# The end of a two-layer encoder: where the last range's squares are added, and what stands behind the last residual sums

## The chip, the core and the metric

The kernel is one program on one NeuronCore of a Trainium2 chip. The metric is the time of one execution in microseconds on the device. Five engines work side by side, each through its own list of instructions in a fixed order: TensorE (PE, with its weight loads shown apart as PEld), VectorE (DVE), ScalarE (ACT), GpSimd (POOL) and SyncE (SP), whose list here holds only the starts of transfers. An instruction that needs another engine's result waits for a semaphore, and everything behind it on its own engine waits with it. TensorE writes its results into PSUM, a small memory of eight banks here; the rest lies in SBUF.

## The reference

Two inputs, a prompt of 256 tokens and a sample of 512, go through the same two layers of width 1024. Layer 0 mixes with an mLSTM in both directions, layer 1 with sliding-window attention; after each mixer comes a gated feed-forward with a convolution of width 3. What matters for this case is the end: the last feed-forward's residual sum, and then the final norm, which is the output.

```python
def rmsnorm(x, g):
    xf = x.astype(jnp.float32)
    y = xf * lax.rsqrt(jnp.mean(xf * xf, axis=-1, keepdims=True) + EPS)
    return (y * g.astype(jnp.float32)).astype(x.dtype)

def trunk(x, c, ...):
    for l in range(DEPTH):
        ...
        h = rmsnorm(x, norm_g[l, 1]) * (1 + sc2) + sh2
        x = x + g2 * conv_ffn(h, ffn_w_up[l], ffn_conv_w[l], ffn_conv_b[l], ffn_w_down[l])
    return rmsnorm(x, final_g)
```

## The kernel before, in words

All 768 tokens are kept transposed: 128 partitions hold a part of the 1024 features, there are eight such parts ("squares" and "tiles" c = 0 to 7 below), and tokens run along the free axis. The residual stream `xt` is two slabs of four parts each (c 0 to 3 in the first, c 4 to 7 in the second). At the end of the last layer the tokens are treated as three ranges of 256: RANGES[0] and RANGES[1] are the sample's halves, and the last one, RANGES[2], is the prompt. I call them the first range, the other range and the last range.

The last stage of the feed-forward's down product (function `down` in `ffn`, with p = NPART - 1) goes through the three ranges. For each c of a range, `tile` makes six matmuls of 128 x 256 (three for each of two chunks of the inner dimension: weights and activations are each split into a high and a low half) into one PSUM bank, and `resid` (L606, VectorE) multiplies them by the gate and adds them to `xt`. `square` (L111, ScalarE) then squares the new `xt`. After the eighth c the range's norm runs as a generator, `Norm.stages`, that is advanced while the next range's tiles are written, by a clock of estimated microseconds (`tick`).

The norm of a range needs the sum of squares over the eight parts and over 128 partitions. The first two ranges add six of the eight squares on VectorE (L120) into one tile; TensorE then sums the remaining three tiles over the partitions by a matmul whose weights are the squares and whose moving operand is two columns of 1/1024 (`inv`). These are the row sums; L136 and L266 in the rows with `pa<-inv,nt`. For the last range nothing is added before: all eight squares go to TensorE one by one (L136). One square's row sum is two matmuls, one for each 128 tokens, and each of them appears as two records in the trace, so four records for a square.

Then a small chain follows. The mean plus epsilon is copied out of PSUM (L159 on VectorE, L157 on ScalarE for the last range), GpSimd raises it to the power -1/2 (L160), and TensorE spreads the factor of each token over all 128 partitions by a product with the identity (`spread`; rows `pa<-kct,nr`, two matmuls and four records). The last range spreads twice, into two banks, so that ScalarE and VectorE each read their own. ScalarE copies the factor to SBUF (L588). Then each of the eight parts is scaled (function `output`): most by one VectorE instruction (L596), the others by ScalarE with the weight g (L593) and by GpSimd with the factor (L594). Each part is stored to HBM when it is scaled (L598): 24 stores of 128 KB, on SP's queue but for four of the last range's, which ScalarE starts.

The `pa` tiles rotate through four PSUM banks, and the `ps` tiles are four more banks that are used in turn. A tile that finds its bank unread must wait for the reader. The order of each engine's list is not the order in which the code is written: a scheduler with a timeline of its own estimates sets it when the program is built, and can put any instruction ahead of another that it doesn't depend on. `issue_after(x)` tells it to put nothing of a block ahead of instruction x.

## Time and profile before

| | us |
|---|---|
| median of 3 runs | 1822.28 |
| lowest and highest of them | 1821.72, 1824.81 |
| profiled execution | 1823.43 |
| its span, first to last instruction | 1821.6 |
| PE busy in it | 1788.2 (98%) |
| DVE busy | 1387.4 (76%) |
| ACT busy | 890.9 (49%) |
| POOL busy | 475.2 (26%) |

The span is 1.83 us shorter than the profiled execution's own time, which also holds what lies ahead of the first and behind the last instruction. TensorE is busy almost throughout, and the change touches only what happens after about 1801 us. So the page's sums say little about it, and the views that follow are those of the last 25 us: the chain of work that ended last, the rows of each engine in order of time, and the busy times by stretch with the clock that TensorE was granted. A row of an engine's timeline has the start in us from the span's start, the time from the first start to the last end, the engine, the line, the operation, what it writes and reads, the shape, and the count; in brackets how long the engine stood idle before it, and what ended that.

### The profile page before, as it was taken

What the parts mean: (1) busy time and instruction counts of PE and PEld (TensorE: products, weight loads), DVE (VectorE), ACT (ScalarE), POOL (GpSimd) and SP (SyncE); (2) the same over time, 40 slices, a digit from 0 to 9 for tenths busy, and PEclk for the clock granted to TensorE, in tenths of its full rate; (3) what the DMA queues carried; (4) which work ended last, traced back from release to release, by engine and by line L of the source; (5) the groups of instructions that cost most, each with busy time, mean ns of one, the idle gap of its engine ahead of it and who ended that gap; (6) DMA issues with size and microseconds to landing.
All of it is one profiled execution on the core that took longest, in us unless ns stands there. A gap on an engine that the chain in (4) does not pass through costs nothing.

```text
span 1821.6 us, 28983 instructions
## 1 busy us (share of the span) xinstructions
PE 1788.2 (98%) x11290; PEld 1653.4 (91%) x11290; DVE 1387.4 (76%) x2148; ACT 890.9 (49%) x1798; POOL 475.2 (26%) x386
## 2 busy tenths in 40 slices
PE   7999999999999999999999999999999999999998
PEld 4988888889998999999999999989989999999997
DVE  4876676786799777787877867767998777777776
ACT  4553343444465444444444657665564444444443
POOL 2100000031024333333331313320244333333321
PEclk9999999999999999999999999999999999999998
DMA  9334565547212122222123321133122222222212
GB/s 339 122 120 147 175 225 172 193 163 228 79 56 81 59 70 70 70 68 66 65 70 95 106 92 42 62 98 128 47 81 70 70 70 70 70 71 70 70 36 70
DMA packets 64245, 184.48 MB, mean 101 GB/s; under 512 B 6167, under 2 KB 23831, under 8 KB 64108
## 3 DMA queue, kind: packets, MB, share of 16 engines
q1 hardware_dynamic: 63532, 182.11, 30.6%
q8 instruction: 89, 1.46, 0.3%
q10 hardware_dynamic: 576, 0.52, 0.1%
q14 instruction: 48, 0.39, 0.1%
HBM read 176.17 MB, written 6.43 MB: 100 GB/s over the span
## 4 chain that ended last, share of the span: by engine, by line
PE 86%; DVE 5%; ACT 4%; DMA 2%; issue 1%; POOL 1%; SPq 0%; POOLq 0%; DVEq 0%; ACTq 0%
PE ps L266 27%; PE pa L266 24%; PE ps L1353 10%; PE ps L1356 10%; PE ps L1354 10%; PE pa L1192 1%; DMA raw<-in_w_dram 1%; ACT whi L272 1%; DVE wlo L273 1%; PE ps L432 1%; DVE ada L528 0%; DMA raw<-in_adaln_w_dram 0%; PE pa L1353 0%; PE pa L1354 0%; DVE wlo L1478 0%
## 5 line engine op out<-in xcount | busy, mean ns | idle before, releaser
L272 ACT CAST whi<-raw 128x1024 fp32r<-128x1024 f32 x231 | 241.8, 1049 | 342.2 <-PE pa L266 143.3
L273 DVE TENSOR_TENSOR wlo<-raw,whi 128x1024 fp32r<-128x1024 f32 x231 | 315.5, 1367 | 114.6 <-ACT whi L272 112.3
L266 PE MATMUL pa<-slab,whi 128*128 128x256 f32 (+1 forms) x1328 | 317.7, 334 | 0.0
L266 PEld LDWEIGHTS pa<-slab,whi 128*128 128x128 f32 x1328 | 230.1, 189 | 21.6 <-DVE slab L606 0.4
L606 DVE SCALAR_TENSOR_TENSOR slab<-pa,mod,slab 128x256 f32<-128x256 f32 (+1 forms) x332 | 192.7, 598 | 63.9 <-PE pa L266 63.8
L266 PE MATMUL pa<-slab,wlo 128*128 128x256 f32 (+1 forms) x664 | 212.7, 333 | 0.0
L266 PE MATMUL ps<-zh,whi 128*128 128x256 f32 (+1 forms) x560 | 188.2, 338 | 0.9 <-ACT whi L272 0.6
L266 PE MATMUL ps<-zl,whi 128*128 128x256 f32 (+1 forms) x560 | 183.9, 331 | 0.5 <-DVE zl L574 0.5
L266 PE MATMUL ps<-zh,wlo 128*128 128x256 f32 (+1 forms) x560 | 181.1, 329 | 0.3 <-DVE wlo L273 0.3
L1353 PE MATMUL ps<-zh,whi 128*128 128x384 f32 x504 | 172.5, 342 | 3.8 <-ACT nt L1424 2.0
L1354 PE MATMUL ps<-zl,whi 128*128 128x384 f32 x504 | 169.9, 337 | 1.8 <-DVE zl L1310 1.8
L1356 PE MATMUL ps<-zh,wlo 128*128 128x384 f32 x504 | 169.2, 336 | 0.0
L266 PE MATMUL ps<-slab,whi 128*128 128x384 f32 (+2 forms) x656 | 163.7, 332 | 0.9 <-DVE slab L273 0.5
L266 PEld LDWEIGHTS pa<-slab,wlo 128*128 128x128 f32 x664 | 125.2, 189 | 13.2 <-DVE wlo L273 0.4
L1389 POOL TENSOR_TENSOR raw<-raw,raw 128x512 f32<-128x512 f32 x40 | 53.6, 1341 | 318.6 <-DVE wlo L273 245.8
L1605 POOL TENSOR_TENSOR slab<-slab 128x772 f32<-128x772 f32 x44 | 86.5, 1967 | 169.2 <-DVE slab L1593 156.0
L1592 DVE SCALAR_TENSOR_TENSOR slab<-slab,cstt,slab 128x771 f32<-128x771 f32 x88 | 106.3, 1210 | 26.6 <-ACT slab L1590 26.4
L266 PEld LDWEIGHTS ps<-zh,whi 128*128 128x128 f32 x560 | 106.5, 190 | 14.0 <-issue 4.4
L528 DVE SCALAR_TENSOR_TENSOR ada<-raw,silc,ada 128x1024 f32<-128x1024 f32 x84 | 109.1, 1333 | 13.0 <-DMA raw<-in_adaln_w_dram 13.0
L266 PEld LDWEIGHTS ps<-slab,whi 128*128 128x128 f32 x656 | 115.3, 188 | 3.4 <-ACT whi L272 0.9
L266 PEld LDWEIGHTS ps<-zl,whi 128*128 128x128 f32 x560 | 106.4, 190 | 12.4 <-issue 3.4
L266 PEld LDWEIGHTS ps<-zh,wlo 128*128 128x128 f32 x560 | 105.3, 190 | 9.6 <-DVE wlo L273 0.5
(305 smaller groups left out, 4302.8 us busy)
## 6 DMA issues: line engine op xcount, KB each, us to landing
raw<-in_w_dram SPq DMA_DIRECT2D x208, 512.0 KB, 3.7
raw<-in_adaln_w_dram SPq DMA_DIRECT2D x84, 512.0 KB, 4.5
slab<-in_x_dram SPq DMA_DIRECT2D x12, 512.0 KB, 7.3
slab<-in_adaln_w_dram SPq DMA_DIRECT2D x12, 512.0 KB, 10.3
slab<-mrows SPq DMA_DIRECT2D x8, 384.0 KB, 4.6
xs<-slab SPq DMA_DIRECT2D x6, 512.0 KB, 3.7
bt<-brow SPq DMA_DIRECT2D x16, 192.0 KB, 3.1
slab<-xs SPq DMA_DIRECT2D x6, 512.0 KB, 6.7
```

The source lines that it names most:

```text
L266: self.nc.tensor.matmul(out, lhsT, rhs, start=start, stop=stop)
L272: nc.scalar.copy(hi, src)
L273: return nc.vector.tensor_tensor(lo, src, hi.bitcast(F32), ALU.subtract)
L432: last = nc.tensor.matmul(ps[r0 : r0 + 32, :], self.silc[:, k, :], cur[:, g * 512 : (g + 1) * 512], start=k == 0, stop=k == KC - 1,)
L528: stt(acc[:, s], row, w, acc[:, s], ALU.mult, ALU.add)
L606: self.nc.vector.scalar_tensor_tensor(x, o, self.mod[l][:, gc + c, q : q + 1], x, ALU.mult, ALU.add)
L1353: mm(o, wh[:, k], hi[k], start=start and k == 0, stop=False, skip_group_check=True)
L1354: mm(o, wh[:, k], lo[k], start=False, stop=False, skip_group_check=True)
L1356: mm(o, wl[:, k], hi[k], start=False, stop=k == 3, skip_group_check=True)
L1389: tt(q[0], q[2], q[0], ALU.subtract)
L1592: stt(y[:, 1:], u[:, :-1], w(0), y[:, 1:], ALU.mult, ALU.add)
L1605: nc.gpsimd.tensor_tensor(y, y, yrow[:, j], ALU.mult)
```

## The change

Four things are changed, all of them in the last layer's last stage.

First, the last range's squares of c = 0 to 3 are added up on GpSimd into one tile (three additions), so that TensorE makes row sums of five tiles instead of eight. Their order is also changed: the squares of c = 5, 6 and 7 are summed first (`begin(3)`), then the added tile and the square of c = 4.

Second, the seventh tile (c = 6) of the last range goes to a `ps` bank instead of a `pa` bank, which moves c = 7 to the next `ps` bank.

Third, the other range's scalings of c = 2 to 7 must not stand ahead of the last range's residual sums of c = 6 and 7 (`self.ends`), and its norm waits longer by the estimates (`gap` 4.5 instead of 2.0, and 1.95 instead of 1.3 between the first two pairs of scalings).

Fourth, the other range's spread must not stand ahead of the last range's third row sum (`self.counted`). The condition for the second spread of the last range is rewritten and still holds for this range alone.

```diff
-    def __init__(self, net, xt, rng, apply, on_pe=2, last=False, adds=None, wait=0.0):
+    def __init__(self, net, xt, rng, apply, on_pe=2, last=False, adds=None, wait=0.0, gap=2.0):
...
         for i in range(self.done, min(n, last + 1)):
             for b, o in enumerate(self.sides):
-                self.net.nc.tensor.matmul(
+                mm = self.net.nc.tensor.matmul(
                     o, self.sums[i][:, b * P : (b + 1) * P], self.net.inv,
                     start=i == b == 0, stop=i == last, skip_group_check=True,
                 )
         self.done = max(self.done, n)
+        return mm
...
-        yield 2.0
+        yield self.gap
         def spread():
             pr = net.pa()[:, : self.n]
-            for b in range(nb):
-                net.mm(pr[:, b * P : (b + 1) * P], r[:, b : b + 1].to_broadcast([P, P]), net.ident, True, True)
+            with ExitStack() as order:
+                if net.counted:
+                    order.enter_context(net.tc.issue_after(net.counted.ins))
+                for b in range(nb):
+                    net.mm(pr[:, b * P : (b + 1) * P], r[:, b : b + 1].to_broadcast([P, P]), net.ident, True, True)
             return pr
         pr = spread()
-        net.twin = spread() if self.on_pe == KC and self.last else None
+        net.twin = spread() if self.on_pe == 4 else None
...
+        self.ends, self.counted = [], None
...
             turn = c in ((2, 5, 7), (0, 2), (2, 5))[2 if end else rng is RANGES[1]]
-            if turn:
...
+            with ExitStack() as order:
+                if rng is RANGES[1] and c > 1:
+                    for ins in self.ends:
+                        order.enter_context(self.tc.issue_after(ins))
+                if turn:
...
-            if c % 2:
+            if rng is RANGES[1] and c == 1:
+                yield 1.95
+            elif c % 2:
                 yield 1.3
...
-                o = (self.ps() if more and c % 2 else self.pa())[:, : s1 - s0]
+                o = (self.ps() if more and (c % 2 or c == KC - 2 and p == NPART - 1 and rng is RANGES[-1]) else self.pa())[:, : s1 - s0]
...
                 norm = Norm(
-                    self, xt, rng, apply, KC if final else 2, final,
-                    None if keep is not None else nc.vector, 0.0 if keep is None or rng is RANGES[-1] else 1.3,
+                    self, xt, rng, apply, 4 if final else 2, final,
+                    None if keep is not None or final else nc.vector, 0.0 if keep is None or rng is RANGES[-1] else 1.3,
+                    4.5 if keep is None and rng is RANGES[1] else 2.0,
                 )
                 for c in range(KC):
-                    tile(ws[c // 4], c, rng, keep is None or rng is not RANGES[-1])
+                    done = tile(ws[c // 4], c, rng, keep is None or rng is not RANGES[-1])
                     norm.square(c)
-                    if final and c > 1:
-                        norm.begin(c - 1)
+                    if final and c >= KC - 2:
+                        self.ends.append(done.ins)
+                    if final and c == KC - 1:
+                        norm.sums = norm.sums[2:] + norm.sums[:2]
+                        self.counted = norm.begin(3)
                     self.tick(0.65)
```

What the scheduler makes of it is seen in the engines' lists. Ahead of these places each engine's list is the same before and after, and behind them only the order at the very end differs. The lines of the changed kernel are numbered higher (L266 is L271, L596 is L605, L606 is L617, L594 is L603, L160 is L161 there; L111, L120 and L136 keep theirs).

On TensorE, where the last range's tiles come to an end, the list before reads as follows. `ps_1271` is its tile of c = 7, `pa_2309` that of c = 2, and `pa_2306` takes the other range's row sums.

```order
L266 MATMUL ps_1271_9914<-slab_2231_16988,whi_2274_17389 128x256 x2
L266 MATMUL ps_1271_9914<-slab_2231_16988,wlo_2275_17390 128x256
L266 MATMUL pa_2306_17594<-inv_81,nt_2289_17482 128x2
L266 MATMUL pa_2309_17613<-slab_2231_16988,whi_2271_17383 128x256 x2
L266 MATMUL pa_2309_17613<-slab_2231_16988,wlo_2272_17384 128x256
L266 MATMUL pa_2309_17613<-slab_2231_16988,whi_2271_17383 128x256 x2
L266 MATMUL pa_2309_17613<-slab_2231_16988,wlo_2272_17384 128x256
L266 MATMUL pa_2306_17594<-inv_81,nt_2302_17563 128x2
L266 MATMUL pa_2306_17594<-inv_81,nt_2303_17577 128x2
```

In the changed kernel the same place of TensorE's list reads as follows; here `ps_1271` is the tile of c = 6, `ps_1272` that of c = 7 and `pa_2312` that of c = 4.

```order
L271 MATMUL ps_1271_9914<-slab_2231_16988,whi_2274_17389 128x256 x2
L271 MATMUL ps_1271_9914<-slab_2231_16988,wlo_2275_17390 128x256
L271 MATMUL ps_1272_9915<-slab_2231_16988,whi_2274_17389 128x256 x2
L271 MATMUL ps_1272_9915<-slab_2231_16988,wlo_2275_17390 128x256
L271 MATMUL ps_1272_9915<-slab_2231_16988,whi_2274_17389 128x256 x2
L271 MATMUL ps_1272_9915<-slab_2231_16988,wlo_2275_17390 128x256
L271 MATMUL pa_2306_17594<-inv_81,nt_2289_17482 128x2
L271 MATMUL pa_2309_17614<-slab_2231_16988,whi_2271_17383 128x256 x2
L271 MATMUL pa_2309_17614<-slab_2231_16988,wlo_2272_17384 128x256
L271 MATMUL pa_2309_17614<-slab_2231_16988,whi_2271_17383 128x256 x2
L271 MATMUL pa_2309_17614<-slab_2231_16988,wlo_2272_17384 128x256
L271 MATMUL pa_2306_17594<-inv_81,nt_2302_17563 128x2
```

One more tile of six matmuls now stands ahead of the row sum that waits for VectorE's last addition, and the tile `pa_2312` follows directly behind the last row shown.

Further on in the same list, before, the row sums of c = 1, 2 and 3 (`pa_2311`), the other range's spread (`pa_2315`), the tile of c = 6 (`pa_2318`) and the remaining four row sums stood in this order:

```order
L136 MATMUL pa_2311_17623<-inv_81,nt_2308_17611 128x2 x2
L136 MATMUL pa_2311_17623<-inv_81,nt_2310_17621 128x2 x2
L136 MATMUL pa_2311_17623<-inv_81,nt_2312_17638 128x2 x2
L266 MATMUL pa_2315_17654<-kct_77,nr_2307_17601 128x128 x2
L266 MATMUL pa_2318_17675<-slab_2231_16988,whi_2274_17389 128x256 x2
L266 MATMUL pa_2318_17675<-slab_2231_16988,wlo_2275_17390 128x256
L266 MATMUL pa_2318_17675<-slab_2231_16988,whi_2274_17389 128x256 x2
L266 MATMUL pa_2318_17675<-slab_2231_16988,wlo_2275_17390 128x256
L136 MATMUL pa_2311_17623<-inv_81,nt_2314_17650 128x2 x2
L136 MATMUL pa_2311_17623<-inv_81,nt_2317_17671 128x2 x2
L136 MATMUL pa_2311_17623<-inv_81,nt_2319_17683 128x2 x2
L136 MATMUL pa_2311_17623<-inv_81,nt_2320_17699 128x2 x2
```

In the changed kernel no tile is left here. TensorE ends with the other range's row sums (`pa_2306`), three row sums of the last range (`pa_2317`: the squares of c = 5, 6 and 7), the other range's spread (`pa_2318`), the two remaining row sums (`nt_2305` is the tile added on GpSimd, `nt_2313` the square of c = 4), and the last range's two spreads:

```order
L271 MATMUL pa_2306_17594<-inv_81,nt_2289_17482 128x2
L271 MATMUL pa_2306_17594<-inv_81,nt_2302_17563 128x2
L271 MATMUL pa_2306_17594<-inv_81,nt_2303_17577 128x2
L136 MATMUL pa_2317_17677<-inv_81,nt_2314_17657 128x2 x2
L136 MATMUL pa_2317_17677<-inv_81,nt_2315_17666 128x2 x2
L136 MATMUL pa_2317_17677<-inv_81,nt_2316_17675 128x2 x2
L271 MATMUL pa_2318_17684<-kct_77,nr_2307_17601 128x128 x2
L136 MATMUL pa_2317_17677<-inv_81,nt_2305_17587 128x2 x2
L136 MATMUL pa_2317_17677<-inv_81,nt_2313_17648 128x2 x2
L271 MATMUL pa_2321_17716<-kct_77,nr_2320_17700 128x128 x2
L271 MATMUL pa_2322_17719<-kct_77,nr_2320_17700 128x128 x2
```

Eight row sums have become five, and the spread stands behind three of them instead of behind four and ahead of the last tile.

On VectorE the end of the list was, before (`pa_2313` and `pa_2318` are the last range's residual sums of c = 4 and c = 6, `pa_2315` the other range's factor, `pa_2322` the last range's):

```order
L606 SCALAR_TENSOR_TENSOR slab_1696_12451<-pa_2309_17613,mod1_89,slab_1696_12451 128x256
L159 TENSOR_SCALAR nr_2307_17601<-pa_2306_17594 128x2
L606 SCALAR_TENSOR_TENSOR slab_1697_12452<-pa_2313_17642,mod1_89,slab_1697_12452 128x256
L596 SCALAR_TENSOR_TENSOR slab_1696_12451<-slab_1696_12451,cstt_75,pa_2315_17654 128x256 x2
L596 SCALAR_TENSOR_TENSOR slab_1697_12452<-slab_1697_12452,cstt_75,pa_2315_17654 128x256 x4
L606 SCALAR_TENSOR_TENSOR slab_1697_12452<-pa_2318_17675,mod1_89,slab_1697_12452 128x256
L596 SCALAR_TENSOR_TENSOR slab_1696_12451<-slab_1696_12451,cstt_75,pa_2322_17720 128x256 x3
```

and is now:

```order
L617 SCALAR_TENSOR_TENSOR slab_1696_12451<-pa_2309_17614,mod1_89,slab_1696_12451 128x256
L617 SCALAR_TENSOR_TENSOR slab_1697_12452<-pa_2312_17640,mod1_89,slab_1697_12452 128x256
L160 TENSOR_SCALAR nr_2307_17601<-pa_2306_17594 128x2
L605 SCALAR_TENSOR_TENSOR slab_1696_12451<-slab_1696_12451,cstt_75,pa_2318_17684 128x256 x2
L605 SCALAR_TENSOR_TENSOR slab_1697_12452<-slab_1697_12452,cstt_75,pa_2318_17684 128x256 x4
L605 SCALAR_TENSOR_TENSOR slab_1696_12451<-slab_1696_12451,cstt_75,pa_2321_17716 128x256 x3
```

No residual sum stands behind the other range's six scalings any more, and the copy of the other range's mean (`nr_2307`) stands behind the last residual sum. On GpSimd the three additions stand ahead of and around that range's power: addition, addition, power, addition, two scalings, the last range's power, two scalings. SP's list and the four stores that ScalarE starts are unchanged.

14 lines of the change are left out of this document (7 added, 7 removed).

## The prediction

> **What bounds the kernel now.** I read the page first, then the chain of waits from 1794 us on, then each engine's timeline from 1801 us on, then busy times with the granted clock.
>
> ```profile
> span 1821.6 us, 28983 instructions
> ...
> PE 86%; DVE 5%; ACT 4%; DMA 2%; issue 1%; POOL 1%; SPq 0%; POOLq 0%; DVEq 0%; ACTq 0%
> ```
>
> TensorE carries 86% of the chain, but none of its work before 1801 us is touched. The chain's end is another matter (start, us, what):
>
> ```profile
> 1808.24 0.91 DVE slab L596 x3
> ...
> 1809.43 1.26 DVE slab L596 x3
> 1810.68 0.40 DVE slab L606
> ...
> 1811.11 0.42 ACT nt L111
> ...
> 1811.58 1.88 PE pa L136 x8
> ...
> 1813.48 0.18 ACT nr L157
> ...
> 1813.73 0.69 POOL nr L160
> ```
>
> The last residual sum (L606) stands behind the other range's six scalings (L596), and square, row sums, mean, power follow one by one. TensorE's rows show what it had ready and for how long it stood:
>
> ```profile
> 1801.22 0.29 PE L266 MATMUL ps<-slab,wlo 128*128 128x256 f32 x1
> 1802.11 0.38 PE L266 MATMUL pa<-inv,nt 128*128 128x2 f32 x2 [0.59 <-DVE nt L120]
> ...
> 1803.15 1.17 PE L266 MATMUL pa<-inv,nt 128*128 128x2 f32 x10
> ...
> 1804.63 0.48 PE L266 MATMUL pa<-slab,whi 128*128 128x256 f32 x2
> ...
> 1805.31 0.28 PE L266 MATMUL pa<-slab,wlo 128*128 128x256 f32 x1
> 1805.43 1.39 PE L136 MATMUL pa<-inv,nt 128*128 128x2 f32 x12
> 1806.68 1.12 PE L266 MATMUL pa<-kct,nr 128*128 128x128 f32 x4
> ...
> 1808.67 0.41 PE L266 MATMUL pa<-slab,wlo 128*128 128x256 f32 x1
> ...
> 1811.58 1.87 PE L136 MATMUL pa<-inv,nt 128*128 128x2 f32 x8 [1.00 <-ACT nt L111]
> 1814.48 2.07 PE L266 MATMUL pa<-kct,nr 128*128 128x128 f32 x8 [1.03 <-POOL nr L160]
> ```
>
> The tile of c = 6 ends at 1809.08 (1808.67 + 0.41), its residual sum starts only at 1810.60 (VectorE's row below). Row sums follow each other at 0.11 us a record early on (1.39 for 12, less one tail) and 0.21 at the end (1.87 for 8). The clock shows why (stretch, length, busy time of PE, PEld, DVE, ACT, POOL; clock; DMA share, GB/s):
>
> ```profile
> 1803.36:1806.78 3.42, 3.42 (x32) 3.42 (x32) 1.29 (x4) 1.77 (x5) 0.70 (x1) 1.00 0.33 115
> 1806.50:1807.00 0.50, 0.50 (x5) 0.50 (x6) 0.00 (x0) 0.06 (x1) 0.00 (x0) 0.78 0.00 0
> 1806.78:1821.60 14.82, 7.74 (x35) 7.27 (x34) 5.27 (x13) 2.46 (x7) 3.51 (x5) 0.50 0.42 143
> ...
> 301.50:304.91 3.41, 3.41 (x8) 2.73 (x9) 3.41 (x3) 0.00 (x0) 0.00 (x0) 0.50 0.96 363
> ```
>
> A mean of 0.78 over 1806.5 to 1807.0 puts the fall to half at 1806.78. It comes at the end of a stretch in which PE was never idle, but did mostly row sums. The only other half-clock stretch is the last row shown.
>
> **The change, part by part.** I first let the clock fall at 1806.78 again.
>
> *Tile of c = 7 moved forward.* Its six matmuls (0.96 us alone: 1804.63 to 1805.59; about 0.12 each in a row) fill the 0.59 us in which TensorE waited for VectorE's last addition. Cost nothing; were the wait gone they would cost 0.7. Everything behind keeps its time up to 1803.15.
>
> *Tile of c = 4 ahead of the row sums.* One two-record sum stands ahead of it, then it takes 1803.29 to 1804.25. VectorE and ScalarE:
>
> ```profile
> 1802.36 0.47 DVE L606 SCALAR_TENSOR_TENSOR slab<-pa,mod,slab 128x256 f32<-128x256 f32 x1
> 1802.76 0.86 DVE L606 SCALAR_TENSOR_TENSOR slab<-ps,mod,slab 128x256 f32<-128x256 f32 x2
> ...
> 1808.24 2.44 DVE L596 SCALAR_TENSOR_TENSOR slab<-slab,cstt,pa 128x256 f32<-128x256 f32 x6 [2.13 <-ACT nt L588]
> 1810.60 0.47 DVE L606 SCALAR_TENSOR_TENSOR slab<-pa,mod,slab 128x256 f32<-128x256 f32 x1
> 1815.74 2.44 DVE L596 SCALAR_TENSOR_TENSOR slab<-slab,cstt,pa 128x256 f32<-128x256 f32 x6 [4.67 <-PE pa L266]
> ...
> 1807.84 0.37 ACT L588 COPY nt<-pa 128x256 f32<-128x256 f32 x1 [1.27 <-PE pa L266]
> ...
> 1811.11 0.72 ACT L111 ACTIVATE nt<-slab 128x256 f32<-128x256 f32 x2 [2.04 <-DVE slab L606]
> ```
>
> VectorE takes a residual sum each 0.39 us (0.86 for two, 0.47 alone): c = 0, 5, 6, 7 from 1802.36, c = 2 at 1803.93, c = 4 from 1804.33 to 1804.80. The last residual sum thus ends 6.3 us earlier than now (1811.07).
>
> *What is late next: the squares.* ScalarE makes one each 0.32 us (0.72 for two): c = 2 at 1804.44, c = 3 at 1804.76, then c = 4, 5, 6, 7, the last from 1806.05 to 1806.45. That is 5.4 us earlier than 1811.83.
>
> *Row sums and spread.* The other range's last eight records, from 1804.09 at 0.11 with a tail of 0.2, end at 1805.04, so its mean is on VectorE at 1805.08 to 1805.23. TensorE then waits for c = 5's square (1805.80), about 0.8 us idle. Twelve records from 1805.85, eight at 0.11 and the rest at 0.21, reach 1807.6. The spread is next in the list, four records at 0.21: 1808.45, result at about 1808.67. Then eight records for the two last tiles, which took 1.87 in the row above: 1808.46 + 1.87 = 1810.3. The row sums before ended at 1813.45. So 3.15 us are left of the 5.4: before, six sums and the spread lay under VectorE's scalings, now they stand in a row. The three row sums that fall away (twelve records, 2.6 us at half clock) are part of these 3.15.
>
> *GpSimd.*
>
> ```profile
> 1804.60 0.70 POOL L160 TENSOR_TENSOR nr<-nr,mhalf 128x2 f32<-128x2 f32 x1 [2.83 <-DVE nr L159]
> 1808.29 1.41 POOL L594 TENSOR_TENSOR slab<-slab,nt 128x256 f32<-128x256 f32 x2 [2.99 <-ACT nt L588]
> ...
> L120 POOL TENSOR_TENSOR nt<-nt,nt 128x256 f32<-128x256 f32 x32 | 25.1, 787 | 42.0 <-ACT nt L111 40.2
> ```
>
> The addition on GpSimd is in the trace from earlier norms: 0.79 us mean, and the scalings of the same shape take 0.70 each; I take 0.73. First addition 1803.67 to 1804.40, second 1804.93 to 1805.67 (it waits for c = 2's square, and the other range's power is queued behind it), power 1805.64 to 1806.34, third addition to 1807.06. TensorE wants the power at 1807.6 and the sum at 1808.46: all hidden, with 1.3 us to spare. Without that cover 0.7 us each would show. The other range's scalings start when ScalarE has copied the factor (0.37): VectorE 1809.11 to 1811.55, GpSimd 1809.16 to 1810.57. The last range's power stands behind these two on GpSimd; its mean is ready at 1810.51, so it waits some 0.05: 1810.59 to 1811.28.
>
> *The end.* Now VectorE's last scalings start 1.26 us after the last spread (1815.74 less 1814.48). That gives 1811.33 + 1.26 = 1812.6, against 1815.74: 3.1 us.
>
> *Stores.* The other range's eight stores start 0.87 later with their scalings (1809.11 against 1808.24), the last range's 3.1 earlier; both are on SP in the same order.
>
> ```profile
> 1809.30:1813.50 4.20, 3.15 (x15) 2.98 (x14) 1.78 (x5) 0.74 (x3) 0.40 (x1) 0.50 0.74 250
> ...
> 1817.00:1820.50 3.50, 0.00 (x0) 0.00 (x0) 1.18 (x4) 0.00 (x0) 1.41 (x2) 0.50 0.88 300
> 1820.50:1821.60 1.10, 0.00 (x0) 0.00 (x0) 0.00 (x0) 0.00 (x0) 0.00 (x0) 0.50 0.00 0
> ```
>
> The first stream, 1813.5 in the row, now ends near 1814.4; the second, 1817.0 in the row, would start near 1813.9. So they touch by half a microsecond. There is no loss if the stores' pace is still set by the scalings that come one by one (2.44 for six), and 0.6 if the second stream starts only behind the first and is never caught up. I take none, since the second stream's 3.5 us are longer than its scalings by one store or two only, and keep 0.6 for the range. The sum is 3.1 us: from the profiled execution's 1823.43 to 1820.3, and from the median, which lies 1.15 below it and inside the same spread, to 1819.2. That is 0.17%; a measurement of this kernel tells about 0.2% (3.64 us) from no change.
>
> **Rivals.** *The clock stays full longer.* 1806.78 less 304.91 is 440 times 3.4133, the length of the half-clock stretch at 301.50. The fall thus comes on a grid that the program does not set; real tiles now end at 1804.25, so it can come anywhere from about 1805.9 to 1809.3. From 1808 on, the sums end at 1808.7 and GpSimd decides: factor at 1807.80, scalings 1808.29 to 1809.70, power (ready 1808.94, 0.75 of wait) to 1810.39, spread, VectorE at 1811.7. That is 4.04 less some 0.3 for the stores: 1818.4. The runs before may have had such falls too, where they gain up to 0.6 of it; the price keeps to the profiled one. If the clock never fell, the spread's four records would give back 0.1 each: 1818.0; I give this 0.05 of the chance below. This last is what the Trainium skill (TensorE: Matmul & The Clock Gate, Part 1) would have: the clock halves only after an idle window of about 3.4 us, and PE idles at most a microsecond here. The trace agrees on the length (3.41) and not on idleness (3.42 of 3.42 us busy before the fall).
>
> *Stores become the bound.* Sixteen stores of 131 KB are 2.1 MB; at 250 GB/s from 1810.1 on (0.87 behind the row's 1809.3) they end at 1818.5, and the 1.1 us without a transfer close the span at 1819.6. Only 2.0 are gained, 1820.3; with a late queue up to 1821. For it: the two streams touch. Against it: 300 GB/s with two queues.
>
> *Slower: GpSimd's power and additions take 1.7 us.* One did so beside a VectorE instruction:
>
> ```profile
> 1022.72 1.70 POOL L160 TENSOR_TENSOR nr<-nr,mhalf 128x2 f32<-128x2 f32 x1
> ...
> 1022.15 1.69 DVE L273 TENSOR_TENSOR wlo<-raw,whi 128x1024 fp32r<-128x1024 f32 x1
> ```
>
> If all seven instructions up to the last power took 1.7: additions 1803.67 to 1807.07, power to 1808.77, third addition to 1810.47, scalings to 1813.87, power to 1815.57, VectorE at 1816.9, that is 1.1 slower: 1823.4. It decides from about 1.45 us an instruction. Against it, L594 took 0.70 beside VectorE's L596 at 1808.29. The Trainium skill (SBUF — State Buffer, Who interferes with whom) says that only a VectorE instruction with two SBUF inputs, or in a two-port mode, blocks GpSimd; the 1.70 agrees (L273 reads raw and whi), and those beside the additions now read one input from PSUM.
>
> **How the numbers follow.** Likeliest 0.46, own range 1818.2 to 1820.2 (the grid's phase and the store's 0.6), 0.18 of it beyond 0.2%. Clock full longer 0.30, all but 0.03 beyond. Stores 0.14, within. Slower 0.10, of which 0.06 beyond 3.64 us, if VectorE's wait adds to it. Faster 0.18 + 0.27 = 0.45; same 0.28 + 0.03 + 0.14 + 0.04 = 0.49; slower 0.06. The range runs from 1817.4 (the clock never falls, and the run's spread below its median, 0.6) to 1821.6 (past the stores); it leaves out the slower case and little else.
>
> **What would show it.** PE's idle 0.59 before the row sum near 1802.1 is gone. The last L617 ends near 1804.8. Squares run from 1804.4 to 1806.5 without a gap. PE idles about 0.8 at 1805. The spread comes behind twelve records, the last eight sums end between 1808.7 and 1810.3, GpSimd's last power starts within 0.1 us of the end of its scalings or of the mean, and VectorE's last six start between 1811.7 and 1812.6. I am wrong if GpSimd's additions take over 1 us, if TensorE waits for one of them, or if the last store ends over 6 us after these scalings start (4.8 now).

## The result, and the profile after

The changed kernel takes 1820.74 us (median of 22 runs, 1817.02 to 1825.20), the kernel before 1822.91 us in the runs beside it (22 runs, 1820.43 to 1828.30). The ratio, taken over all the runs, is 0.9984, with a 95% interval of 0.9977 to 0.9990. That is 2.9 us of 1822.9 (the two medians alone lie 2.2 us apart), a small gain whose interval ends on both sides of 0.2%. A second set of runs of the same kernel (below) gave 0.9975 (0.9966 to 0.9985). The forecast was 0.17%. The profiled execution took 1818.95 us. Its page:

```profile
span 1817.1 us, 28967 instructions
...
PE 87%; DVE 5%; ACT 4%; DMA 2%; issue 1%; POOL 1%; SPq 0%; POOLq 0%; ACTq 0%; DVEq 0%
```

Runs of one and the same kernel lie up to 8 us apart, and the parts here are worth 0.3 to 4 us, so I read the end of the program by itself. As a mark I take the last addition of squares on VectorE; it is the same instruction in every kernel, and in all of them VectorE's list over the 40 us ahead of it is the same, with the same times to 0.07 us when counted from it. In the kernel before it starts here (start, us, what):

```profile
1801.55 0.50 DVE L120 TENSOR_TENSOR nt<-nt,nt 128x256 f32<-128x256 f32 x1
```

From there to the end of the span are 20.1 us (1821.6 less 1801.55). I call this length "the tail". The timelines of VectorE, ScalarE and GpSimd in the changed kernel:

```profile
1800.57 0.52 DVE L120 TENSOR_TENSOR nt<-nt,nt 128x256 f32<-128x256 f32 x1
...
1801.80 1.25 DVE L617 SCALAR_TENSOR_TENSOR slab<-ps,mod,slab 128x256 f32<-128x256 f32 x3
1802.97 0.86 DVE L617 SCALAR_TENSOR_TENSOR slab<-pa,mod,slab 128x256 f32<-128x256 f32 x2
...
1807.42 2.44 DVE L605 SCALAR_TENSOR_TENSOR slab<-slab,cstt,pa 128x256 f32<-128x256 f32 x6 [3.15 <-ACT nt L593]
1810.85 2.44 DVE L605 SCALAR_TENSOR_TENSOR slab<-slab,cstt,pa 128x256 f32<-128x256 f32 x6 [0.99 <-PE pa L271]
...
1803.54 1.95 ACT L111 ACTIVATE nt<-slab 128x256 f32<-128x256 f32 x6 [0.90 <-DVE slab L617]
...
1808.25 0.17 ACT L158 ACTIVATE nr<-pa 128x2 f32<-128x2 f32 x1 [0.86 <-PE pa L136]
...
1805.46 0.73 POOL L120 TENSOR_TENSOR nt<-nt,nt 128x256 f32<-128x256 f32 x1
1807.46 1.40 POOL L603 TENSOR_TENSOR slab<-slab,nt 128x256 f32<-128x256 f32 x2 [1.27 <-ACT nt L593]
1808.83 0.70 POOL L161 TENSOR_TENSOR nr<-nr,mhalf 128x2 f32<-128x2 f32 x1
```

The tail is 16.5 us (1817.1 less 1800.57), 3.6 shorter. The two spans differ by 4.5; the other 1.0 lies ahead of the mark and is not the change's. The last residual sum (L617) now ends 3.26 us behind the mark, where it ended 9.5 behind it; the squares follow without a gap. The mean (L158) is ready at 1808.42, and the power (L161) starts only at 1808.83, behind GpSimd's two scalings. TensorE:

```profile
1801.14 0.38 PE L271 MATMUL pa<-inv,nt 128*128 128x2 f32 x2
...
1804.93 1.50 PE L136 MATMUL pa<-inv,nt 128*128 128x2 f32 x12 [0.86 <-ACT nt L111]
1806.29 0.69 PE L271 MATMUL pa<-kct,nr 128*128 128x128 f32 x4
1806.81 1.40 PE L136 MATMUL pa<-inv,nt 128*128 128x2 f32 x8
1809.58 2.08 PE L271 MATMUL pa<-kct,nr 128*128 128x128 f32 x8 [1.37 <-POOL nr L161]
```

The wait of 0.59 us ahead of the first row sum is gone, one of 0.86 has come for the squares. The chain of waits from there on runs over GpSimd's scalings (L603) to the power:

```profile
1804.93 1.50 PE pa L136 x12
1806.43 0.57 PE pa L271 x4
...
1807.46 1.40 POOL slab L603 x2
1808.87 0.66 POOL nr L161
```

The last view of the changed kernel gives busy times by stretch (its last three columns: granted clock, DMA share, GB/s). The clock fell later than in the profile before: 6.6 us behind the mark, not 5.2. The half-clock stretch at 301.5 did not come at all in this execution:

```profile
1803.73:1807.15 3.42, 2.56 (x24) 2.48 (x23) 0.27 (x2) 2.69 (x9) 2.09 (x3) 1.00 0.02 8
1807.15:1817.10 9.95, 3.14 (x14) 2.76 (x13) 4.88 (x12) 0.78 (x3) 3.47 (x5) 0.50 0.63 211
301.50:304.91 3.41, 2.50 (x11) 1.85 (x11) 3.12 (x7) 0.71 (x1) 0.00 (x0) 1.00 0.96 351
```

So two executions with different falls of the clock stand side by side here, and the first question of the experiments is how much of the 3.6 us belongs to the change.

### The profile page after: what moved, and what is told of

It is laid out like the page before. It is cut to its first block, busy times and chain, and to the rows that moved or that the text cites. A ratio compares the mean times of both kernels' runs of the same rounds, so it can differ in the third digit from the quotient of the medians.

```text
span 1817.1 us, 28967 instructions
## 1 busy us (share of the span) xinstructions
PE 1784.3 (98%) x11278; PEld 1649.3 (91%) x11278; DVE 1387.0 (76%) x2148; ACT 890.3 (49%) x1798; POOL 478.3 (26%) x389
## 4 chain that ended last, share of the span: by engine, by line
PE 87%; DVE 5%; ACT 4%; DMA 2%; issue 1%; POOL 1%; SPq 0%; POOLq 0%; ACTq 0%; DVEq 0%
PE ps L271 27%; PE pa L271 24%; PE ps L1364 11%; PE ps L1367 10%; PE ps L1365 10%; PE pa L1203 1%; DMA raw<-in_w_dram 1%; DVE wlo L278 1%; PE ps L437 1%; ACT whi L277 1%; DVE ada L533 0%; PE pa L1365 0%; PE pa L1364 0%; DVE wlo L1489 0%; PE pa L1367 0%
## 5 line engine op out<-in xcount | busy, mean ns | idle before, releaser
L271 PE MATMUL pa<-slab,whi 128*128 128x256 f32 (+1 forms) x1324 | 316.2, 334 | 0.0
L271 PEld LDWEIGHTS pa<-slab,whi 128*128 128x128 f32 x1324 | 229.0, 188 | 21.6 <-DVE slab L617 0.4
L617 DVE SCALAR_TENSOR_TENSOR slab<-pa,mod,slab 128x256 f32<-128x256 f32 (+1 forms) x331 | 192.1, 598 | 62.7 <-PE pa L271 62.5
L271 PE MATMUL pa<-slab,wlo 128*128 128x256 f32 (+1 forms) x662 | 211.9, 332 | 0.0
L271 PE MATMUL ps<-zh,whi 128*128 128x256 f32 (+1 forms) x560 | 187.6, 337 | 0.9 <-ACT whi L277 0.6
L271 PE MATMUL ps<-zl,whi 128*128 128x256 f32 (+1 forms) x560 | 183.5, 330 | 0.5 <-DVE zl L579 0.5
L271 PE MATMUL ps<-zh,wlo 128*128 128x256 f32 (+1 forms) x560 | 180.5, 328 | 0.6 <-DVE wlo L278 0.6
L271 PE MATMUL ps<-slab,whi 128*128 128x384 f32 (+2 forms) x660 | 164.4, 332 | 0.8 <-DVE slab L278 0.5
L271 PEld LDWEIGHTS pa<-slab,wlo 128*128 128x128 f32 x662 | 124.6, 188 | 13.2 <-DVE wlo L278 0.4
L271 PEld LDWEIGHTS ps<-slab,whi 128*128 128x128 f32 x660 | 115.9, 188 | 3.4 <-ACT whi L277 0.9
L271 PEld LDWEIGHTS ps<-zh,whi 128*128 128x128 f32 x560 | 106.1, 190 | 13.9 <-issue 3.9
L271 PEld LDWEIGHTS ps<-zl,whi 128*128 128x128 f32 x560 | 106.0, 190 | 12.2 <-issue 3.4
L271 PEld LDWEIGHTS ps<-zh,wlo 128*128 128x128 f32 x560 | 105.0, 189 | 10.1 <-DVE wlo L278 1.0
```

Of the source, the lines that this page charges most:

```text
L271: self.nc.tensor.matmul(out, lhsT, rhs, start=start, stop=stop)
L617: return self.nc.vector.scalar_tensor_tensor(x, o, self.mod[l][:, gc + c, q : q + 1], x, ALU.mult, ALU.add)
```

## The experiments

All kernels in one table. "Tail" is the span's end less the start of the last L120 on VectorE; "fall" is where the granted clock went to half, counted from the same mark. The ratio is to the kernel before in the same set of runs.

| Kernel | Median us (runs) | Ratio, 95% interval | Tail us | Fall us |
|---|---|---|---|---|
| before | 1822.91 (22) | | 20.1 | 5.2 |
| changed | 1820.74 (22) | 0.9984 (0.9977 to 0.9990) | 16.5 | 6.6 |
| order alone | 1819.86 (11) | 0.9985 (0.9976 to 0.9994) | 16.8 | 7.7 |
| additions alone | 1824.07 (11) | 1.0003 (0.9994 to 1.0013) | 21.2 | 4.4 |
| no scalings on GpSimd | 1819.50 (11) | 0.9983 (0.9974 to 0.9991) | 18.1 | 4.5 |
| changed, wide sums | 1819.03 (11) | 0.9981 (0.9973 to 0.9990) | 16.4 | 13.0 |
| before, wide sums | 1820.08 (12) | 0.9981 (0.9971 to 0.9991) | 17.6 | 15.4 |
| before, wide sums, same order | 1821.54 (11) | 0.9989 (0.9980 to 0.9998) | 18.4 | 15.9 |
| order alone, wide sums | 1819.42 (12) | 0.9977 (0.9968 to 0.9986) | 16.7 | 10.8 |
| wide sums, power first | 1819.80 (8) | 0.9977 (0.9967 to 0.9987) | 16.4 | 11.2 |
| the same, stores on two queues | 1818.63 (5) | 0.9970 (0.9958 to 0.9982) | 15.7 | 12.9 |
| the same, spread earlier | 1819.68 (12) | 0.9978 (0.9969 to 0.9986) | 16.5 | 10.9 |
| the same, GpSimd ahead of the power | 1818.82 (5) | 0.9967 (0.9955 to 0.9979) | 15.9 | 11.1 |
| changed, again | 1820.88 (10) | 0.9975 (0.9966 to 0.9985) | 16.5 | 6.8 |

**Order alone.** GpSimd's additions are taken out; the order is kept.

```diff
...
-                    self, xt, rng, apply, 4 if final else 2, final,
+                    self, xt, rng, apply, KC if final else 2, final,
...
-                        norm.sums = norm.sums[2:] + norm.sums[:2]
-                        self.counted = norm.begin(3)
+                        self.counted = norm.begin(KC - 2)
```

> The changed kernel without GpSimd's additions: all eight squares of the last range are summed on TensorE (six sums ahead of the other range's spread, two behind it), the other range's scalings still behind the last residual sum. Theory A (the gain is the order: the last residual sum ahead of the scalings; the additions only take row sums out of the way): twelve records more stand ahead of the spread; four to eight of them fit into TensorE's wait for a square (0.86 us in the changed kernel), the rest costs 0.11 us each at full clock or 0.21 at half. So it is 0.5 to 1.6 us slower than the changed kernel, some 1821.2 to 1822.3 where the changed one has 1820.7 and the one before 1822.9, and in the profile the last L617 still ends ahead of the first L605 of the other range. Theory B (the gain is the three row sums that leave TensorE): all of the gain is lost, 1822.9 or more. Theory C (TensorE has room, the additions are worth nothing): 1820.7.

The tail is 16.8 us, 0.3 longer than that of the changed kernel, and the ratio is the same within its interval. Theory B (the row sums that leave TensorE are the gain) is out: with all of them back nearly all of the gain stays. From TensorE's timeline in this kernel:

```profile
1804.21 2.82 PE L136 MATMUL pa<-inv,nt 128*128 128x2 f32 x24
```

The twelve more records start 1.0 earlier than the twelve of the changed kernel (3.35 against 4.36 us behind the mark, where that one waits 0.86 for a square) and run at full clock; only 0.3 comes out at the end. My range began at 0.5. The clock fell 1.1 us later in this execution than in the changed kernel's, but in both behind the other range's spread, on which the scalings wait, so the fall hardly touches the 0.3.

**Additions alone.** The kernel before, with the additions on GpSimd and the row sums still begun tile by tile.

```diff
...
-                    self, xt, rng, apply, KC if final else 2, final,
-                    None if keep is not None else nc.vector, 0.0 if keep is None or rng is RANGES[-1] else 1.3,
+                    self, xt, rng, apply, 4 if final else 2, final,
+                    None if keep is not None or final else nc.vector, 0.0 if keep is None or rng is RANGES[-1] else 1.3,
...
-                    if final and c > 1:
-                        norm.begin(c - 1)
+                    if final and c > 3:
+                        norm.begin(c - 3)
```

> The kernel before with the additions alone: the last range's first four squares are added on GpSimd, its row sums are still begun tile by tile, and the other range's six scalings on VectorE still stand ahead of the last residual sum. Theory A: no gain. The first row sum now needs the third addition (about 1807.1 on the clock of the profile before) and stands ahead of the spread on TensorE, which starts after it: the spread ends some 0.5 to 0.9 us later than the 1807.80 of before, the scalings, the last residual sum and the end with it: 1823.4 to 1823.8 where the kernel before has 1822.9. Theory B (row sums taken from TensorE are the gain): twelve records less at half clock, up to 2.5 us faster, 1820.4.

No gain; the tail is 1.1 us longer than that of the kernel before. From the timelines of TensorE and GpSimd in this kernel:

```profile
1809.03 1.01 PE L136 MATMUL pa<-inv,nt 128*128 128x2 f32 x4 [1.78 <-POOL nt L120]
...
1808.25 0.72 POOL L120 TENSOR_TENSOR nt<-nt,nt 128x256 f32<-128x256 f32 x1
```

TensorE waits 1.78 us for the third addition, with the spread behind it in its list. The additions are harmless in the changed kernel because their sum stands behind the spread there, not because they are short. (The clock fell 0.8 earlier here than in the profile before, so not all of the 1.1 is the addition's.)

**No scalings on GpSimd.** All eight scalings of the other range go to VectorE.

```diff
-            turn = c in ((2, 5, 7), (0, 2), (2, 5))[2 if end else rng is RANGES[1]]
+            turn = c in ((2, 5, 7), (), (2, 5))[2 if end else rng is RANGES[1]]
```

> The changed kernel with all eight scalings of the other range on VectorE, none on GpSimd. Theory D (GpSimd now decides: the last range's power waits for its two scalings, 1808.42 to 1808.83 in the profile of the changed kernel): the power starts within 0.1 us of the mean; VectorE is then busy with eight scalings until about 1810.6 and starts the last ones at 1810.5 to 1810.6 instead of 1810.85. Gain 0.3 us, less what the stores take: 1820.4 to 1820.7. Theory E (the stores decide the end, SP issues one in 0.49 us without a pause): no gain at all, with the same time from the last scalings' start to the end plus 0.3.

From this kernel's timelines of TensorE and GpSimd:

```profile
1805.67 2.61 PE L136 MATMUL pa<-inv,nt 128*128 128x2 f32 x12 [0.85 <-ACT nt L111]
...
1809.14 1.71 PE L136 MATMUL pa<-inv,nt 128*128 128x2 f32 x8
...
1811.13 0.71 POOL L161 TENSOR_TENSOR nr<-nr,mhalf 128x2 f32<-128x2 f32 x1 [4.20 <-ACT nr L158]
```

and from its busy times by stretch, on either side of the clock's fall (third column from the right):

```profile
1802.42:1805.83 3.41, 2.56 (x24) 2.47 (x22) 2.32 (x7) 2.27 (x7) 1.72 (x3) 1.00 0.50 171
1805.83:1809.24 3.41, 3.41 (x18) 3.41 (x18) 0.00 (x0) 1.20 (x4) 1.10 (x2) 0.50 0.00 0
```

The power now waits for its mean alone (L158), as theory D has it, but what this is worth can't be read here: the clock fell 0.16 us after the first row sum began, and the tail became 18.1. What the run does show is the early fall itself. The twelve records took 2.61 us where they took 1.50, and the eight sums end 9.5 us behind the mark (1809.14 + 1.71 less 1801.34), where they ended at 7.6.

**Wide sums.** If the row sums let the clock fall because two columns leave TensorE's array unused, sums of 128 columns should keep it up. The two columns of 1/D become a tile of ones; 1/D moves into the step that adds epsilon.

```diff
...
-                    o, self.sums[i][:, b * P : (b + 1) * P], self.net.inv,
+                    o, self.sums[i][:, b * P : (b + 1) * P], self.net.inv if self.w == 2 else self.net.ones,
...
-            nc.scalar.activation(r, mean, AF.Copy, bias=EPS)
+            nc.scalar.activation(r, mean, AF.Copy, bias=EPS, scale=k)
...
+                if keep is None and rng is not RANGES[0]:
+                    norm.w = P
```

> The changed kernel with the row sums of the last two norms made 128 columns wide (a tile of ones in place of two columns of 1/D, the factor 1/D moved into the step that adds epsilon), so that TensorE streams in every record. The spread's records of 128 columns took 0.11 us at full clock, as the two-column sums do, so the sums themselves should not get longer by more than 0.02 us a record. Theory F (the clock falls because the two-column sums leave TensorE's array unused): the granted clock stays at 1.00 to the last spread, the last eight sum records end in 0.9 to 1.0 us instead of 1.40, the last range's factor takes 0.5 for four records instead of about 1.0; the power still waits for GpSimd's scalings, so 0.4 to 0.5 us of this reach the end: 1820.2 to 1820.4. Theory G (the clock falls at a fixed point whatever TensorE streams): the fall comes at the same place and the time stays 1820.7.

Busy times by stretch in this kernel, from the row sums on in the second row (clock third from the right):

```profile
1804.31:1808.09 3.78, 3.02 (x25) 2.83 (x24) 2.85 (x8) 2.38 (x8) 1.56 (x3) 1.00 0.57 192
1808.09:1813.92 5.83, 4.10 (x32) 3.72 (x32) 2.86 (x8) 1.90 (x6) 3.35 (x5) 1.00 0.27 91
```

and its timelines of TensorE and VectorE (its mark is at 1803.74):

```profile
1808.09 1.60 PE L138 MATMUL pa<-ones,nt 128*128 128x128 f32 x12 [0.76 <-ACT nt L111]
...
1809.98 1.06 PE L138 MATMUL pa<-ones,nt 128*128 128x128 f32 x8
1812.76 1.16 PE L274 MATMUL pa<-kct,nr 128*128 128x128 f32 x8 [1.72 <-POOL nr L164]
...
1813.50 2.44 DVE L608 SCALAR_TENSOR_TENSOR slab<-slab,cstt,pa 128x256 f32<-128x256 f32 x6 [0.48 <-PE pa L274]
```

Theory F's forecast came, and theory G's did not. The clock is full to the last factor, although TensorE was busy for only 4.10 of the 5.83 us and stood still for 1.72 of them at one stretch; eight sums take 1.06 instead of 1.40, the last factor's eight records 1.16 instead of 2.08. Over all kernels: in the six profiles with two-column sums the fall came 4.4 to 7.7 us behind the mark, ahead of the last factor in each; in the eight with wide sums it came at 10.8 to 15.9, when TensorE had no more work. The records got hardly longer (1.60 against 1.50 for twelve). One thing stays open: with the width the values went from 1/1024 to 1, and neither was varied by itself.

In the changed kernel this is worth 0.1 us of the tail, 0.3 to 0.4 less than I expected. The last scalings start 0.5 earlier behind the mark (9.76, where they started at 10.28), but the end does not follow: from there to the end of the span are 6.6 us, where they are 6.2 in the changed kernel and 5.9 in the one before. The stores take the rest, of which more below.

**The kernel before with wide sums, twice.** This sets the two kernels side by side without a fall of the clock.

> The kernel before with the row sums of its last two norms 128 columns wide, as in the changed kernel with wide sums, so that both can be set side by side without the fall of the clock. I count from the start of VectorE's last addition of squares (1801.55 in the profile before) to the end of the span: 20.1 us before, 16.5 changed, 16.4 changed with wide sums. If the clock stays full: spread 0.5 instead of 1.12, last eight sums 1.0 instead of 1.87, last factor 0.5 instead of 1.0: 18.1 to 18.3. The gain of the change at full clock is then 1.8, of 3.6 between the two profiled executions, and the rest of those 3.6 is the clock's fall at another point. Rival (the change's gain is the same 3.6 whatever the clock does): 20.0. Where TensorE waits 1 to 2.5 us for the last residual sum the share of streaming gets low again, so the clock may fall there; then 18.6 to 19.2. Median 1.5 below that of the kernel before, 1821.5.

17.6, below my 18.1 to 18.3. Its timeline on VectorE shows why; the scheduler had let the last residual sum ahead of two of the six scalings:

```profile
1811.61 1.66 DVE L599 SCALAR_TENSOR_TENSOR slab<-slab,cstt,pa 128x256 f32<-128x256 f32 x4 [1.71 <-ACT nt L591]
1813.18 0.48 DVE L609 SCALAR_TENSOR_TENSOR slab<-pa,mod,slab 128x256 f32<-128x256 f32 x1
```

So the old order was put back by hand:

```diff
...
-                self.resid(xt, o, l, 40, c, rng)
+                with ExitStack() as order:
+                    if keep is None and c == KC - 2 and rng is RANGES[-1] and p == NPART - 1:
+                        self.ready(RANGES[1])
+                        order.enter_context(self.tc.issue_after(self.lastscale.ins))
+                    self.resid(xt, o, l, 40, c, rng)
```

> The kernel before with wide sums, with the last residual sum held behind all six of the other range's scalings on VectorE, as in the kernel before; with wide sums alone it had moved ahead of two of them (17.6 us from the last addition of squares to the end). Two scalings at 0.39 us: 18.3 to 18.4. Then the change is worth 1.9 to 2.0 us at full clock (16.4 changed), and what the two profiled executions show beyond that, 3.6, is the fall of the clock. If the time stays at 17.6, the order on VectorE was not what the change gained by.

From VectorE's timeline (the mark is at 1799.96):

```profile
1806.22 2.44 DVE L599 SCALAR_TENSOR_TENSOR slab<-slab,cstt,pa 128x256 f32<-128x256 f32 x6 [1.70 <-ACT nt L591]
1808.57 0.48 DVE L609 SCALAR_TENSOR_TENSOR slab<-pa,mod,slab 128x256 f32<-128x256 f32 x1
1812.50 2.44 DVE L599 SCALAR_TENSOR_TENSOR slab<-slab,cstt,pa 128x256 f32<-128x256 f32 x6 [3.44 <-PE pa L269]
```

18.4 us: two scalings moved ahead of one residual sum cost 0.8, two times 0.39. This measures the mechanism of the change by itself, and at full clock the change is worth 2.0 us (18.36 less 16.39). VectorE's last scalings even start 2.8 us earlier with the change (12.54 us behind the mark here, 9.76 in the changed kernel with wide sums); the stores take 0.8 of that, since 5.8 us follow to the end here and 6.6 there. If the wide sums do nothing but keep the clock up, its fall cost the profiled kernel before 1.7 (20.09 less 18.36) and the changed one 0.1, where the stores hide most of it.

Each of these tails is one execution. The medians of whole runs are too coarse to confirm the 2.0: the ratios to the kernel before are 0.9981 for the changed kernel with wide sums, 0.9981 for the kernel before with them and 0.9989 for the one in the old order, with intervals that overlap.

**Order alone, with wide sums.**

> The order alone (all eight squares summed on TensorE, none added on GpSimd) with wide sums. It prices GpSimd's additions without the fall of the clock. With two-column sums, where the clock fell only behind the spread, the kernel without additions was 0.3 us longer from the last addition of squares to the end (16.8 against 16.5). Theory A: again 0.3 to 0.5 us longer than the changed kernel with wide sums, 16.7 to 16.9: twelve records of 0.11 us, of which the 0.76 us of TensorE's wait take seven. Theory C (nothing): 16.4.

16.7, that is 0.3 more than with the additions. At full clock they are worth 0.3 us, as in the pair with two-column sums.

**Power first.** Wide sums, and GpSimd's two scalings of the other range (now those of c = 6 and 7) go behind the power.

```diff
...
-            turn = c in ((2, 5, 7), (0, 2), (2, 5))[2 if end else rng is RANGES[1]]
+            turn = c in ((2, 5, 7), (6, 7), (2, 5))[2 if end else rng is RANGES[1]]
...
+                    if rng is RANGES[1]:
+                        order.enter_context(self.tc.issue_after(self.lastpow.ins))
                     nc.gpsimd.tensor_tensor(x(c), x(c), side, ALU.mult)
```

> The changed kernel with wide sums, and the other range's two GpSimd scalings are those of c = 6 and 7 and stand behind the last range's power. Theory D (GpSimd's two scalings in front of the power decide): with wide sums the mean was ready 7.5 us after the last addition of squares, the power started at 8.25. Here it starts within 0.1 us of the mean, the factor is spread by 8.9, and VectorE, which has six scalings until 9.3, starts the last six there instead of at 9.76: 0.4 to 0.5 us less, 16.0 in place of 16.4. Theory E (stores decide the end): the last six start earlier by the same, but 16.3 to 16.4 stay.

From this kernel's timelines of VectorE and GpSimd:

```profile
1808.76 4.79 DVE L612 SCALAR_TENSOR_TENSOR slab<-slab,cstt,pa 128x256 f32<-128x256 f32 x12 [2.99 <-ACT nt L598]
...
1809.50 0.71 POOL L164 TENSOR_TENSOR nr<-nr,mhalf 128x2 f32<-128x2 f32 x1 [1.96 <-ACT nr L161]
```

and from its busy times by stretch (DMA share and GB/s at the right):

```profile
1810.00:1813.00 3.00, 1.16 (x8) 0.97 (x8) 3.00 (x9) 0.37 (x1) 2.63 (x5) 1.00 0.69 232
1813.00:1817.00 4.00, 0.00 (x0) 0.00 (x0) 0.55 (x2) 0.00 (x0) 0.37 (x1) 0.52 0.99 340
```

Theory D is right about the engines and theory E about the end. The power starts with its mean, VectorE runs its twelve scalings without a pause and begins the last six 0.6 us earlier; the tail stays at 16.4, where theory D had 16.0. The transfers move 232 GB/s while there are scalings and 340 for four microseconds after them.

**Stores on two queues.**

```diff
-            queue = nc.scalar if end and c in (1, 2, 5, 7) else nc.sync
+            queue = nc.scalar if c in (2, 5, 7) and end or c in (2, 4) and rng is RANGES[1] else nc.sync
```

> As the one before, and the other range's stores of c = 2 and 4 go to ScalarE's queue, the last range's of c = 1 to SP. Theory E (SP issues one store in 0.49 us without a pause and its last one comes 13.1 us after the last addition of squares): SP's last issue comes 0.5 to 1.0 us earlier, and the end with it: 15.5 to 15.9. Theory H (the transfers themselves decide, at 340 GB/s in the last 2 us): no more than 0.2 from the queue, 15.8 to 16.0. If ScalarE's copy of the factor is held behind its stores, GpSimd's last scalings come late and it is 16.2.

The same view of this kernel:

```profile
1810.00:1812.00 2.00, 0.54 (x5) 0.34 (x4) 2.00 (x6) 0.37 (x1) 1.63 (x4) 1.00 1.01 341
1812.00:1814.00 2.00, 0.00 (x0) 0.00 (x0) 0.67 (x2) 0.00 (x0) 0.49 (x1) 0.99 1.02 341
```

15.7 us, in theory E's range: SP's last issue starts 12.3 us behind the mark, 13.2 in the kernel before this one. But the DMA engines are now full from early on, at 341 GB/s, so the transfers themselves, theory H's case, come next. The Trainium skill (DMA: Bandwidth & Descriptors, Specifications) puts one core's share of HBM at about 358 GB/s; the rows lie 5% below that, and no run here shows what sets them. That figure is no ceiling for this core in general: loads moved 363 GB/s in the profile before (301.50 to 304.91, in the prediction). Of the kernels tried this tail is the shortest, 0.8 below the changed kernel's; the ratio of 0.9970 points the same way, but its interval overlaps with that of the changed kernel.

**Spread earlier.** The change puts the other range's spread behind three row sums of the last range; here it stands behind one.

```diff
...
-                        self.counted = norm.begin(3)
+                        self.counted = norm.begin(1)
```

(with the other sums held behind the spread). In the second kernel GpSimd takes c = 2 and 4 ahead of the power.

> As the kernel with the power first and two stores on ScalarE's queue (15.7 us from the last addition of squares to the end), but the other range's factor is spread on TensorE behind one row sum of the last range instead of three. Its power ends 4.8 us after that addition, the first sum's four records at about the same point. Theory I (where the changed kernel puts the spread costs it the start of the scalings, and with it of the stores): the scalings start at 5.8 to 5.9 instead of 6.76, the last range's sums end no later, since TensorE's wait only moves, and its six scalings start at 8.8 to 8.9 instead of 9.12. The transfers ran at 340 GB/s from the first store to the last, so they end 0.7 to 0.9 earlier: 14.8 to 15.0. Rival (the end hangs on the last scalings, not on the transfers): 0.2 to 0.3 earlier, 15.4 to 15.5.

> As the one before, and GpSimd takes the other range's c = 2 and 4 in the time before the last range's power, which the earlier scalings now leave free; ScalarE's queue has the stores of c = 2 and 7. All eight scalings of the other range then end at about 8.3 after the last addition of squares, where GpSimd's two behind the power end at 9.6. If the transfers have gaps in the middle because those two come late, this closes them: 14.6 to 14.9. If the power has to wait behind GpSimd's second scaling by more than 0.3 us, the last six scalings start at 9.2 or later and it is 15.0 to 15.2.

Both missed. The scalings started 0.7 us earlier (I had expected 0.9), but the last six did not (9.19 and 9.20 behind the mark, 9.12 without), and the tails got longer, 16.5 and 15.9. The last six wait for the last range's factor, and its row sums ended no earlier: 7.4 behind the mark in both, 7.2 without. In the first the transfers broke off in the middle (busy times by stretch, DMA share and GB/s at the right):

```profile
1810.00:1811.00 1.00, 0.00 (x0) 0.00 (x0) 0.99 (x3) 0.00 (x0) 0.91 (x2) 0.63 0.80 259
1811.00:1812.00 1.00, 0.00 (x0) 0.00 (x0) 0.00 (x0) 0.00 (x0) 0.00 (x0) 0.50 0.41 134
```

One of its issues on SP took four times as long as the others (the instructions of the stores' line: min, median and max in ns):

```profile
L618 SPq DMA_DIRECT2D out_dram<-slab x11: 332/381/1526, 1805.9 to 1812.7; - x11
```

In the second the same happened near the start; the same two views of it:

```profile
1808.00:1809.00 1.00, 0.55 (x5) 0.56 (x6) 0.49 (x2) 0.00 (x0) 0.39 (x1) 1.00 0.24 74
```

```profile
L616 SPq DMA_DIRECT2D out_dram<-slab x11: 332/402/1540, 1806.6 to 1812.5; - x11
```

Whether the earlier spread is worth anything is thus open: the start of the stores did move, and a long issue of 1.5 us stood in each of the two. In every other profile of this study the longest issue of a store is 0.69 us or less, and these are one execution each. The Trainium skill (Perfetto Trace Analysis, DMA Instruction — HWDGE (DVE, Sync)) has the issuing engines share one block that makes descriptors, which each locks; in the first kernel ScalarE finished a store (10.89 to 11.23 us behind the mark) while SP's long one ran (10.69 to 12.22), so that lock alone does not explain it.

**The changed kernel again.**

> The changed kernel once more, unchanged, for another fall of the clock and beside the others in the same runs. By the clock alone: where it falls 6.6 us or more after the last addition of squares, 16.4 to 16.6 from there to the end; where it falls at 4.5, as in the kernel with all scalings on VectorE, 18.0 to 18.2; where between, a value between, some 0.7 us for each microsecond. If the time is 16.5 with an early fall as well, the 18.1 of that kernel came from its scalings and not from the clock.

The fall came at 6.8 us and the tail is 16.5 us, as in the first profile. So in this pair the tail repeats to a few hundredths when the fall does to 0.2 us. An execution of this kernel with an early fall was not caught.

## Why the prediction was right, and where not

It forecast 3.1 us and 1819.2 from a median of 1822.28. The ratio 0.9984 makes 1819.4 of that median, the second set's 0.9975 makes 1817.7, and the range held both. The steps, counted from the mark:

- *Tile of c = 7 forward, free:* right, the wait of 0.59 is gone.
- *Last residual sum:* 3.25 us predicted, 3.26 measured (1803.83).
- *Squares:* the last one to end at 4.90, measured 4.92 (1803.54 + 1.95 less 1800.57).
- *TensorE's wait:* 0.8 predicted, 0.86 measured; the row sums begin at 4.30, measured 4.36.
- *From the row sums on* the profile went the way of the rival that I had given 0.30, "the clock stays full longer". The sums end at 7.64 (rival 7.15, likeliest case 8.75). The power waits 0.41 behind GpSimd's scalings (rival 0.75, likeliest 0.05). VectorE's last scalings start at 10.28 (rival 10.15, likeliest 11.05). The likeliest case fits its own clock: where the fall came 0.7 us earlier still, in the kernel without scalings on GpSimd, the eight sums end at 9.5, and 0.65 of the difference to 8.75 would be the half clock on six and a half more records (0.21 instead of 0.11 each).
- *GpSimd:* 0.73 an addition, as predicted, so the slower rival did not come. (The 1.45 us from which it was to decide does not follow from the prediction's times: seven instructions from 1803.67 reach the power's forecast end of 1811.28 at 1.09 us each. And the rival with the later fall sums to 1818.5, not 1818.4.) The spare is smaller than the 1.3 us I gave: the third addition ends at 1806.19 and TensorE reaches the next sums at 1806.81, 0.6 later.
- *"The three row sums that fall away (twelve records, 2.6 us at half clock) are part of these 3.15":* this is the sentence that failed. The kernels without additions show 0.3 us for it, with the clock falling late or not at all. Most of the twelve records fit into TensorE's wait for the squares, 0.86 us that stand empty in the changed kernel. With an early fall they may cost more; that was not measured.
- *Stores:* none in the forecast, 0.3 in the rival, 0.6 in the range. Measured is 0.3: 5.9 us from the start of VectorE's last scalings to the end before, 6.2 after. At full clock it is 0.8, and the rival that has them become the bound came true once the last scalings were made earlier still.

The mechanism was right, the last residual sum ahead of the scalings; that its size came out so near was in part luck. The profile's 3.6 us are not all the change's: 2.0 are left at full clock, and 1.6 come from a clock that fell on more of the old tail than of the new one (1.7 against 0.1). I had priced the change against one profiled fall as if every run had it, and named the phase of the fall as a rival; it is a part of both times. Some of the 1.6 may be the change's own doing, since less of TensorE's list is left to be slowed, and some the phase of the two executions; no run separates the two. Over many runs the gain is 2.9 (the first set) or 4.6 us (the second), and these data don't divide it further.

## What to carry to other kernels

When a chain ends in small steps on several engines, look for the one engine that has work of another chain in front of the step that all wait for; the new order, which puts six scalings behind one residual sum, gave 1.7 us of the 2.0 here (18.36 less 16.70, with wide sums; the bank, the place of the spread and the longer wait were not tried apart from it), and taking work off the engine that looked busy gave 0.3. Compare two profiles of a tail only at the same clock: make the clock the same (here by wider sums) or read the part where it matters out of both. Then ask what stands next; here it was GpSimd's order, then the stores.

## What the runs showed of the hardware

- The clock of TensorE fell although it was busy all the time (3.42 of 3.42 us before the fall in the profile before), and did not fall where it was busy for 4.10 of 5.83 us, nor in the kernel before with wide sums and the old order, where two stretches of 3.41 us one behind the other (1805.61 to 1812.43) hold 1.77 and 1.84 us of work. What differed was the width of the row sums: two columns or 128, at about the same 0.11 us a record (and the values, 1/1024 or 1). Width is not the whole rule: at 301.50 the profile before fell behind a stretch of 3.41 us in which TensorE was busy for 2.10, with matmuls of 128 to 512 columns. The Trainium skill (TensorE: Matmul & The Clock Gate, Part 1) ties the fall to idle windows of about 3.4 us; by that none of these fourteen tails should have seen a fall before its last factor, and six did.
- Sixteen stores of 131 KB move at 230 to 270 GB/s while one queue issues most of them (one in 0.49 us: 250 before, 270 changed, 232 with the power first), and at 288 to 341 where ScalarE issues some of them too.
- Twice, of the 22 issues in the two kernels with the earlier spread, SP took 1.5 us to issue one store instead of 0.4. Its cause is open.
